# The two MLPs in an order written out by hand, with half of one more weight block as a Strassen product

## The chip, the cores and the metric

The kernel runs on one core of a Trainium2 chip. The metric is device time in microseconds: the median over executions of the whole kernel, inputs and outputs in HBM. Beside it there is a profile of one execution, from which all rows below are taken. The engines are called as the profile calls them: PE is TensorE (matmuls; PEld its weight loads), DVE VectorE, ACT ScalarE, POOL GpSimd, SP SyncE, which issues the loads.

## The reference

A model of two layers on 256 tokens of width 2048, all in fp32. Each layer adds an attention and then an MLP to the residual h: layer 0 a stick-breaking attention, layer 1 a native sparse attention with compressed, selected and windowed branches. The change concerns the MLPs alone:

```python
def sqrelu_mlp(h, w1, w2):
    return jnp.square(jax.nn.relu(h @ w1)) @ w2

h = h + sqrelu_mlp(rms_norm(h, mlp_norm_g[layer]), mlp_w1[layer], mlp_w2[layer])
```

w1 is 2048 x 8192, w2 is 8192 x 2048.

## The kernel before

**Precision.** A product in fp32 is made of three matmuls in fp32r. Each operand is split into a high part (a copy to fp32r, on ACT) and a low part (the difference, on DVE), and high x high, low x high and high x low are summed in PSUM. So each chunk of weights, 256 rows by 512 columns, 512 KB, is loaded to a `raw` tile by SP (`load`), split by ACT and DVE into `hi` and `lo` (`split`, lines 142 and 144; four buffers of each), and used by PE.

**Chunks.** Three kinds are told apart below. A chunk of the first product (`chunk_T`, line 206, "T") has 24 matmuls of 256 columns: the weights are the stationary operand, the normalized input xs (its halves xhi and xlo) moves. A plain chunk of the second product (`chunk_N`, line 173, "N") has 12 matmuls of 512 columns: the activations yhi and ylo are stationary, the weights move. A Strassen chunk of the second product (`chunk_S`, line 269, "S") does the same with seven half-size products instead of eight: 21 matmuls of 256 columns. For it DVE forms three sums of quarters of the weights (lines 245, 248, 249), ACT and DVE split three of the quarters (`shi` and `slo`, one buffer each, lines 247 and 250) and the four sums (lines 142 and 144 again). The activations' sums `ss` are made once, when the activations are made. The products of one S block fill four PSUM banks; `add_S` combines them into h with one ACT copy and seven DVE instructions (lines 293 to 302).

**Groups.** An MLP runs in four groups of 2048 hidden columns. In each, `group1` makes 32 T chunks (four blocks of 512 hidden columns, eight chunks each) and after each block the squared relu, its split into yhi and ylo, and the sums `ss`. Then `group2` multiplies by the matching rows of w2, in four blocks of 512 output columns: blocks 0 and 1 as N chunks, with block 2's eight S chunks put between them. Block 3's eight S chunks are put between the T chunks of the next group. In the last group blocks 0, 1 and 3 are plain and block 2 is S.

**Residual inputs.** When a block of h is finished, `next_x` prepares the next layer's input from it. It is a generator: first the squares of the block on ACT (`ssq`, line 349), then twice `make_x`: four transposes on PE (line 328), two ACT copies to xhi (line 333), two DVE instructions to xlo (line 335). `spawn` puts such a generator on a list with a rate, and `pump`, which each chunk calls twice (behind its hi matmuls and behind its lo matmuls), adds half the rate to a count and takes a step for every whole one. After the output projection of an attention, the `next_x` of its last block is still on that list when the MLP begins. `done` adds them at the end of layer 0's MLP; at the end of layer 1 it stores finished blocks of the output.

**Order.** Every engine runs its instructions in the order of its own queue. In most of the kernel the framework's scheduler chooses that order, from its own estimate of when things are ready, and may put an instruction ahead of others that the program emits earlier. In a block `with tc.manual_schedule(engines=...)` the order on the named engines is that in which the program emits. The kernel has one such block, the first stage (lines 508 to 571), where the first projections start; both MLPs are left to the scheduler.

**Loads.** `raw` tiles rotate over five buffers; within the MLPs every sixth load uses one more, `raw6`.

## Time and profile before

| | |
|---|---|
| median of 3 runs | 2145.69 us (2145.44 to 2146.96) |
| the profiled execution | 2144.79 us, of which its span is 2143.1 us |
| PE busy | 2136.4 us, 100% of the span |
| DVE busy | 1563.9 us, 73% |
| ACT busy | 1231.6 us, 57% |
| DMA | 190 GB/s mean |
| granted PE clock | 1.00 |

The MLP of layer 0 runs on PE from 391.7 us of the span, that of layer 1 from 1459.0 us to the end. In rows of a timeline the first number is the start and the second the length, in us; "x24" is a count of merged instructions, and a bracket gives the idle time before an instruction and what ended it. In rows of waits the numbers are the total, the count and the longest. Rows of the chain of waits have start, length, engine, tile and line.

### The profile page before, as it was taken

Reading aid. Unit: us, or ns where it says so; the run is one execution under the profiler, and the core shown is the slowest. Engines: PE = TensorE matmul, PEld = TensorE weight load, DVE = VectorE, ACT = ScalarE, POOL = GpSimd, SP = SyncE. Lnnn points to the kernel's source line nnn. Section 1 sums busy time; section 2 is a strip of 40 time slices with the busy share of each in tenths; the row PEclk is TensorE's granted clock in tenths of the full one; section 3 lists DMA queues with packets and bytes.
Section 4 is the critical chain, followed back from the end, with each engine's and each line's share of the span. In section 5 each row is a group of like instructions: output and inputs, shape, how many; then the busy total and the mean of one; then the engine's idle time right before and its main releaser. Section 6 shows DMA issues by size and latency. Waiting matters only on the chain.

```text
span 2143.1 us, 37272 instructions
## 1 busy us (share of the span) xinstructions
PE 2136.4 (100%) x14894; PEld 1973.4 (92%) x14894; DVE 1563.9 (73%) x2131; ACT 1231.6 (57%) x1653; POOL 45.2 (2%) x75
## 2 busy tenths in 40 slices
PE   9999999999999999999999999999999999999999
PEld 9999988998998999999898888889989989989998
DVE  5556556567878778778777888765678797788786
ACT  6555665555555555565555666655655555655653
POOL 0000000000000000000000111000000000000000
PEclk9999999999999999999999999999999999999999
DMA  7655556665665666665667654456656656656664
GB/s 240 210 172 177 158 180 186 186 195 188 207 202 186 205 197 203 217 197 186 194 185 217 169 145 136 149 177 187 197 170 215 205 188 213 197 189 210 204 195 149
DMA packets 260789, 406.34 MB, mean 190 GB/s; under 512 B 13188, under 2 KB 91912, under 8 KB 260616
## 3 DMA queue, kind: packets, MB, share of 16 engines
q1 hardware_dynamic: 259800, 403.52, 60.2%
q8 instruction: 116, 1.90, 0.4%
q10 hardware_dynamic: 816, 0.46, 0.1%
q14 instruction: 57, 0.47, 0.1%
HBM read 401.83 MB, written 2.10 MB: 188 GB/s over the span
## 4 chain that ended last, share of the span: by engine, by line
PE 98%; DVE 1%; DMA 0%; ACT 0%; issue 0%; POOL 0%; SPq 0%; DVEq 0%; ACTq 0%; POOLq 0%
PE acc L206 43%; PE acc L173 37%; PE att L269 12%; PE att L173 1%; PE att L328 1%; PE att L944 1%; DMA raw<-in_nsa_w_in_dram 0%; DVE lo L144 0%; PE att L655 0%; PE att L607 0%; PE att L882 0%; PE att L938 0%; PE att L884 0%; PE att L883 0%; PE att L936 0%; PE att L937 0%
## 5 line engine op out<-in xcount | busy, mean ns | idle before, releaser
L142 ACT ACTIVATE hi<-raw 128x1024 fp32r<-128x1024 f32 x639 | 676.0, 1060 | 576.1 <-PE acc L206 274.0
L144 DVE TENSOR_TENSOR lo<-raw,hi 128x1024 fp32r<-128x1024 f32 x639 | 776.6, 1222 | 252.9 <-ACT hi L142 241.3
L206 PE MATMUL acc<-xs,hi 128*128 128x256 f32 x5360 | 665.2, 277 | 0.0
L206 PEld LDWEIGHTS acc<-xs,hi 128*128 128x128 f32 x5360 | 634.4, 188 | 0.9
L206 PE MATMUL acc<-xs,lo 128*128 128x256 f32 x2680 | 359.3, 277 | 0.0
L206 PEld LDWEIGHTS acc<-xs,lo 128*128 128x128 f32 x2680 | 329.2, 188 | 0.0
L173 PE MATMUL acc<-hi,yhi 128*128 128x512 f32 x828 | 324.9, 393 | 0.0
L173 PE MATMUL acc<-hi,ylo 128*128 128x512 f32 x828 | 323.4, 391 | 0.0
L173 PE MATMUL acc<-lo,yhi 128*128 128x512 f32 x828 | 224.3, 392 | 0.0
L245 DVE TENSOR_TENSOR ts<-raw 128x512 f32<-128x512 f32 x112 | 77.4, 691 | 167.2 <-DMA raw<-in_mlp_w_dram 166.7
L142 ACT ACTIVATE hi<-ts 128x1024 fp32r<-128x1024 f32 x112 | 118.7, 1060 | 136.8 <-PE acc L173 67.8
L173 PEld LDWEIGHTS acc<-lo,yhi 128*128 128x128 f32 x828 | 154.7, 188 | 31.6
L173 PEld LDWEIGHTS acc<-hi,ylo 128*128 128x128 f32 x828 | 155.7, 188 | 29.5 <-DVE ylo L315 0.2
L173 PEld LDWEIGHTS acc<-hi,yhi 128*128 128x128 f32 x828 | 155.6, 188 | 29.5 <-ACT yhi L314 0.2
L173 PE MATMUL acc<-hi,xs 128*128 128x512 f32 x704 | 177.2, 392 | 0.0
L173 PEld LDWEIGHTS acc<-hi,xs 128*128 128x128 f32 x704 | 130.3, 188 | 26.1
L144 DVE TENSOR_TENSOR lo<-ts,hi 128x1024 fp32r<-128x1024 f32 x112 | 136.5, 1219 | 3.5 <-ACT hi L142 3.5
L247 ACT ACTIVATE shi<-raw 128x768 fp32r<-128x768 f32 x112 | 94.6, 845 | 54.8 <-PE att L269 34.5
L250 DVE TENSOR_TENSOR slo<-raw,shi 128x768 fp32r<-128x768 f32 x112 | 106.7, 953 | 4.8 <-PE att L269 4.8
L173 PE MATMUL acc<-lo,xs 128*128 128x512 f32 x352 | 97.1, 396 | 0.0
L269 PE MATMUL att<-hi,ss 128*128 128x256 f32 x672 | 94.4, 276 | 0.0
L269 PEld LDWEIGHTS att<-hi,ss 128*128 128x128 f32 x672 | 84.5, 188 | 0.0
(248 smaller groups left out, 2119.7 us busy)
## 6 DMA issues: line engine op xcount, KB each, us to landing
raw<-in_mlp_w_dram SPq DMA_DIRECT2D x512, 512.0 KB, 4.3
raw<-in_sb_w_qkv_dram SPq DMA_DIRECT2D x95, 512.0 KB, 3.9
raw<-in_nsa_w_in_dram SPq DMA_DIRECT2D x50, 512.0 KB, 3.8
raw<-in_sb_w_out_dram SPq DMA_DIRECT2D x32, 512.0 KB, 3.9
raw<-in_nsa_w_in_dram SPq DMA_DIRECT2D x64, 256.0 KB, 3.8
raw<-in_nsa_w_out_dram SPq DMA_DIRECT2D x32, 512.0 KB, 3.6
w1t<-in_nsa_cmp_w_dram SPq DMA_DIRECT2D x8, 512.0 KB, 4.0
h<-in_x_dram SPq DMA_DIRECT2D x8, 256.0 KB, 4.5
```

Of the source, the lines that this page charges most:

```text
L142: nc.scalar.activation(hi, raw, AF.Copy)
L144: nc.vector.tensor_tensor(lo, raw, hi.bitcast(F32), op=OP.subtract)
L173: mm = lambda a, b, k, t, s, e: nc.tensor.matmul(ps[t], a[:, k, t * P:(t + 1) * P], b, start=s, stop=e)
L206: nc.tensor.matmul(o, w, x[:, k0 + kk, :], start=s, stop=e, skip_group_check=True)
L245: nc.vector.tensor_tensor(ts[:, :2, :], flat[:, W:3 * W].rearrange("p (a n) -> p a n", a=2), b12, op=OP.subtract)
L247: nc.scalar.activation(hi, flat[:, :3 * W], AF.Copy)
L250: nc.vector.tensor_tensor(lo, flat[:, :3 * W], hi.bitcast(F32), op=OP.subtract)
L269: nc.tensor.matmul(ps[i], a, w, start=s, stop=e, skip_group_check=True)
L328: nc.tensor.transpose(ps[:, j * T + t * P:j * T + (t + 1) * P], h[:, t, (kp + j) * P:(kp + j + 1) * P], ident)
L944: nc.tensor.transpose(ptp[:w, j * P:(j + 1) * P], src(j), ident)
```

## The change

Both MLPs are put into a block of hand-written order. `group1` and `group2` with their generator give way to a list of steps (`plan`): chunks T, N and S, and the evaluations that belong to them, placed by the index of the plain chunk behind which they come. The evaluation of a block of hidden columns becomes four steps behind successive chunks: relu and square; the copy to yhi with the four DVE sums; the copy of the sums with ylo; the low half of the sums. A group but the last now has in its second half 20 plain chunks (block 0's eight N, the first block of the next group's T chunks, block 1's last four N) and 12 S chunks (block 1's first four, block 2's eight), and in its first half 24 T chunks beside block 3's eight S chunks. The last group keeps blocks 0, 1 and 3 plain and block 2 S. Block 1 therefore has two sums into h, one of each kind. Three further buffers take three of every eight loads (`more`), so raw tiles rotate over eight. The square is computed in place of the relu, the Strassen sum's temporary shares a buffer with the activations' sums, the squares' scratch tile has one buffer, and three output stores of layer 1 are issued from POOL instead of SP. `pump`, `chunk_T`, `chunk_N`, `chunk_S`, `make_x` and `next_x` stay as they are.

The functions that are taken away are those shown above; their bodies are left out here.

```diff
--- before.py
+++ after.py
@@ -35,6 +35,7 @@
 ST = 32
 SK = 2 * ST + NCMP
 GATES = 3 * NH
+JUNK = 1
 SLOPES = [2.0 ** (-8.0 * (i + 1) / NH) for i in range(NH)]
 
 
@@ -144,14 +145,14 @@
         nc.vector.tensor_tensor(lo, raw, hi.bitcast(F32), op=OP.subtract)
         return hi, lo
 
-    sixth = None
+    more = None
     loads = 0
 
     def load(src, k0, nk, n0, nn):
         nonlocal loads
         loads += 1
-        if sixth is not None and loads % 6 == 0:
-            raw = sixth.tile([P, nk, nn], F32, name="raw6", bufs=1)
+        if more is not None and loads % 8 in (2, 5, 7):
+            raw = more.tile([P, nk, nn], F32, tag="more", name="more", bufs=3)
         else:
             raw = wraw.tile([P, nk, nn], F32, tag="raw", name="raw")
         nc.sync.dma_start(
@@ -287,7 +288,7 @@
     def add_S(nb, bs, ps, pool, scale):
 
         W = NB // 2
-        uv = pool.tile([P, 4, W], F32, tag="pre", name="uv", bufs=1)
+        uv = pool.tile([P, 4, W], F32, tag="sums", name="uv", bufs=1)
         u, v = uv[:, :2, :], uv[:, 2:, :]
         hb = [h[:, t, nb * NB:(nb + 1) * NB] for t in range(NT)]
         nc.scalar.activation(u[:, 0, :], ps[0], AF.Copy)
@@ -345,7 +346,7 @@
             ssq_t[layer] = small.tile([P, NT, n], F32, tag="ssq", name="ssq")
         w = D // n
         for t in range(NT):
-            j = small.tile([P, NB], F32, tag="junk", name="junk")
+            j = small.tile([P, NB], F32, tag="junk", name="junk", bufs=JUNK)
             nc.scalar.activation(
                 j[:, :w], h[:, t, i * w:(i + 1) * w], AF.Square, accum_out=ssq_t[layer][:, t, i:i + 1]
             )
@@ -417,80 +418,159 @@
     def mlp(l, layer, junk, done, last=None):
         w1, w2 = mlp_w1[l], mlp_w2[l]
         ss = far(junk, KD * 4 * P, "ss").rearrange("p (a k i n) -> p a k i n", a=2, k=KD // 2, i=4)
-        factor = junk.tile([P, T], F32, name="factor", bufs=1)[:, :NT]
+        factor = junk.tile([P, 64], F32, name="factor", bufs=1)[:, :NT]
+        NK, NF, NG, KB = KD // KC, D // NB, DFF // D, NB // P
+        banks, part = {}, {}
 
         def factors():
             yield
             r = make_rstd(layer)
             nc.vector.tensor_tensor(factor, r, r, op=OP.mult)
 
-        def in_S(fg, nb):
...
-        def group1(fg, beside_w1):
...
-        def group2(fg, end):
...
+        def chunk1(fg, fb, i):
+            if i == 0:
+                banks["T", fb] = [bank(acc, "acc") for _ in range(KB // 2)]
+            chunk_T(banks["T", fb], w1, i * KC, fg * D + fb * NB, i == 0, i == NK - 1)
+
+        def relu(fb):
+            a = part["s", fb] = junk.tile([P, KB, T], F32, tag="sq", name="sq", bufs=1)
+            for j in range(0, KB, 2):
+                nc.scalar.activation(
+                    a[:, j:j + 2, :], banks["T", fb][j // 2].rearrange("p (m t) -> p m t", m=2), AF.Relu
+                )
+
+        def square(fb):
+            s = part["s", fb]
+            nc.scalar.activation(s, s, AF.Square)
+
+        def high(fb):
+            k, s = fb * KB, part["s", fb]
+            nc.scalar.activation(yhi[:, k:k + KB, :], s, AF.Copy)
+            sv = s.rearrange("p (j kk) t -> p j kk t", kk=2)
+            a1, a2 = [[sv[:, :, kk, t * P:(t + 1) * P] for kk in (1, 0)] for t in range(NT)]
+            q = part["q", fb] = junk.tile([P, 2, 4, P], F32, tag="sums", name="sums", bufs=1)
+            nc.vector.scalar_tensor_tensor(q[:, :, 0, :], a2[0], -1.0, a2[1], op0=OP.mult, op1=OP.subtract)
+            nc.vector.tensor_tensor(q[:, :, 2, :], a1[0], a2[0], op=OP.subtract)
+            nc.vector.tensor_tensor(q[:, :, 1, :], a2[1], q[:, :, 2, :], op=OP.subtract)
+            nc.vector.tensor_tensor(q[:, :, 3, :], a1[1], q[:, :, 1, :], op=OP.subtract)
+
+        def low(fb):
+            k, s = fb * KB, part["s", fb]
+            nc.scalar.activation(ss[:, 0, k // 2:k // 2 + 2], part["q", fb], AF.Copy)
+            nc.vector.tensor_tensor(ylo[:, k:k + KB, :], s, yhi[:, k:k + KB, :].bitcast(F32), op=OP.subtract)
+
+        def low7(fb):
+            k = fb * KB
+            o = ss[:, :, k // 2:k // 2 + 2]
+            nc.vector.tensor_tensor(o[:, 1], part["q", fb], o[:, 0].bitcast(F32), op=OP.subtract)
+
+        def chunk2(fg, nb, i, first, end, turn, by_token=False):
+            if first:
+                banks["N", nb] = [bank(acc, "acc") for _ in range(NT)]
+            chunk_N(banks["N", nb], w2, fg * KD + i * KC, nb * NB, first, end, yhi, ylo, koff=fg * KD,
+                    by_token=by_token, turn=turn)
+
+        def chunk7(fg, nb, i, first, end):
+            if first:
+                banks["S", nb] = banks_S(att, "att")
+            chunk_S(banks["S", nb][1], w2, fg * KD + i * KC, nb * NB, first, end, yhi, ylo, ss[:, 0], ss[:, 1],
+                    koff=fg * KD)
+
+        def sum2(nb):
+            add_h(nb, banks["N", nb], factor)
+
+        def sum7(nb):
+            add_S(nb, *banks["S", nb], junk, factor)
+
+        def plan():
+
+
+            def merge(plain, after):
+                for j, c in enumerate(plain):
+                    yield c
+                    yield from after.pop(j, ())
+                assert not after
+
+            def do(f, *args):
+                return lambda: f(*args)
+
+            def Ts(fg, fb):
+                return [("T", fg, fb, i) for i in range(NK)]
+
+            def Ns(fg, nb, ks=range(NK)):
+                return [("N", fg, nb, i, i == ks[0], i == ks[-1]) for i in ks]
+
+            def Ss(fg, nb, at, after, ks=range(NK)):
+                for i, j in zip(ks, at):
+                    after.setdefault(j, []).append(("S", fg, nb, i, i == ks[0], i == ks[-1]))
+
+            def put(after, j, *fs):
+                after.setdefault(j, []).extend(fs)
+
+            def stages(after, j, fb, stash=False):
+                if not stash:
+                    put(after, j, do(relu, fb))
+                put(after, j, do(square, fb))
+                for i, f in enumerate((high, low, low7)):
+                    put(after, j + 1 + i, do(f, fb))
+
+            half = NK // 2
+            for fg in range(NG):
+                after = {}
+                if fg == 0:
+                    plain = sum([Ts(0, fb) for fb in range(NF)], [])
+                    for fb in range(NF - 1):
+                        stages(after, fb * NK + NK + 2, fb)
+                else:
+                    plain = sum([Ts(fg, fb) for fb in range(1, NF)], [])
+                    put(after, 2, do(sum7, 2))
+                    put(after, 3, do(sum2, 1))
+                    Ss(fg - 1, 3, (3, 5, 7, 10, 13, 15, 18, 21), after)
+                    stages(after, 8, 0, True)
+                    stages(after, 13, 1)
+                    stages(after, 18, 2)
+                yield from merge(plain, after)
+                after = {}
+                if fg:
+                    put(after, 1, do(sum7, 3))
+                stages(after, 2, NF - 1)
+                if fg < NG - 1:
+                    plain = Ns(fg, 0) + Ts(fg + 1, 0) + Ns(fg, 1, range(half, NK))
+                    Ss(fg, 1, (4, 5, 6, 7), after, range(half))
+                    put(after, 10, do(sum7, 1))
+                    put(after, 11, do(sum2, 0))
+                    Ss(fg, 2, (12, 13, 14, 15, 16, 17, 18, 19), after)
+                    put(after, 18, do(relu, 0))
+                else:
+                    plain = Ns(fg, 0) + Ns(fg, 1) + Ns(fg, 3)
+                    put(after, 10, do(sum2, 0))
+                    Ss(fg, 2, (4, 6, 8, 10, 11, 13, 15, 17), after)
+                    put(after, 17, do(sum2, 1))
+                    put(after, 18, do(sum7, 2), *[do(done, n, (att, "att")) for n in range(3)])
+                    if last is None:
+                        put(after, 23, do(sum2, 3), do(done, 3, (att, "att")))
+                yield from merge(plain, after)
 
         spawn(factors(), 1)
-        NK = KD // KC
-        for fg in range(DFF // D):
-            group1(fg, in_S(fg - 1, 3) if fg else None)
-            group2(fg, fg == DFF // D - 1)
+        with tc.manual_schedule(engines={mybir.EngineType.PE, mybir.EngineType.DVE, mybir.EngineType.Activation,
+                                         mybir.EngineType.SP}):
+            steps = list(plan())
+            for n, c in enumerate(steps):
+                if callable(c):
+                    c()
+                    continue
+                follower = next((d[0] for d in steps[n + 1:] if not callable(d)), None)
+                if c[0] == "T":
+                    chunk1(*c[1:])
+                elif c[0] == "S":
+                    chunk7(*c[1:])
+                elif last is not None and c[1:3] == (NG - 1, 3):
+                    fg, nb, i, first, end = c[1:]
+                    chunk2(fg, nb, i, first, i == NK - 2, False, end)
+                else:
+                    chunk2(*c[1:], turn=follower in ("T", "S"))
+            if last is not None:
+                add_out(3, banks["N", 3], last, factor)
 
 
     with tc.tile_pool(name="sbp", bufs=2) as sp:
@@ -690,13 +770,13 @@
     nc.vector.tensor_copy(peT, ppe[:, :2 * CL])
 
     with tc.tile_pool(name="m0p", bufs=2) as mp:
-        wsum = sixth = mp
+        wsum = more = mp
 
         def done0(nb, pool):
             spawn(next_x("nsa", nb, G_NSA, pool), 1.5)
 
         mlp(0, "m0", mp, done0)
-        sixth = None
+        more = None
 
 
 
@@ -842,7 +922,7 @@
 
         def heads(pv, t, n):
 
-            sq = small.tile([P, n, P], F32, tag="junk", name="hsq")
+            sq = small.tile([P, n, P], F32, tag="junk", name="hsq", bufs=JUNK)
             nc.scalar.activation(sq, pv, AF.Square, scale=rstd[:, t:t + 1])
             s = small.tile([P, HG], F32, tag="hs", name="hs", bufs=4)
             nc.vector.tensor_reduce(s[:, :n], sq, axis=AX.X, op=OP.add)
@@ -1082,12 +1162,12 @@
         out_proj(nsa_w_out[0], "m1", G_M1)
 
     with tc.tile_pool(name="m1p", bufs=2) as mp:
-        wsum = sixth = mp
+        wsum = more = mp
         ov = out[0].rearrange("(t p) d -> p t d", p=P)
 
         def done1(nb, pool):
             if nb < D // NB - 1:
-                nc.sync.dma_start(ov[:, :, nb * NB:(nb + 1) * NB], h[:, :, nb * NB:(nb + 1) * NB])
+                nc.gpsimd.dma_start(ov[:, :, nb * NB:(nb + 1) * NB], h[:, :, nb * NB:(nb + 1) * NB])
 
         mlp(1, "m1", mp, done1, ov)
```

More of the change, by code (lines that the diff above doesn't have):

```diff
@@ L425, in factors @@
             nc.vector.tensor_tensor(factor, r, r, op=OP.mult)
-        def in_S(fg, nb):
-            for i in range(NK):
-                if i == 0:
-                    bs, s = banks_S(att, "att")
-                chunk_S(s, w2, fg * KD + i * KC, nb * NB, i == 0, i == NK - 1, yhi, ylo, ss[:, 0], ss[:, 1],
-                        koff=fg * KD)
-                if i == NK - 1:
-                    add_S(nb, bs, s, junk, factor)
-                yield
-        def group1(fg, beside_w1):
-            step = lambda: next(beside_w1)
-            for fb in range(D // NB):
-                ps = [bank(acc, "acc") for _ in range(NB // P // 2)]
-                proj_T(ps, w1, fg * D + fb * NB, then={2: step, 5: step} if beside_w1 else {})
-                k, n = fb * (NB // P), NB // P
-                a = junk.tile([P, n, T], F32, tag="pre", name="pre", bufs=1)
-                for j in range(0, n, 2):
-                    nc.scalar.activation(a[:, j:j + 2, :], ps[j // 2].rearrange("p (m t) -> p m t", m=2), AF.Relu)
-                s = junk.tile([P, n, T], F32, tag="sq", name="sq", bufs=1)
-                nc.scalar.activation(s, a, AF.Square)
-                nc.scalar.activation(yhi[:, k:k + n, :], s, AF.Copy)
-                nc.vector.tensor_tensor(ylo[:, k:k + n, :], s, yhi[:, k:k + n, :].bitcast(F32), op=OP.subtract)
-                sv = s.rearrange("p (j kk) t -> p j kk t", kk=2)
-                a1, a2 = [[sv[:, :, kk, t * P:(t + 1) * P] for kk in (1, 0)] for t in range(NT)]
-                q = junk.tile([P, 2, 4, P], F32, tag="sums", name="sums", bufs=1)
-                nc.vector.scalar_tensor_tensor(q[:, :, 0, :], a2[0], -1.0, a2[1], op0=OP.mult, op1=OP.subtract)
-                nc.vector.tensor_tensor(q[:, :, 2, :], a1[0], a2[0], op=OP.subtract)
-                nc.vector.tensor_tensor(q[:, :, 1, :], a2[1], q[:, :, 2, :], op=OP.subtract)
-                nc.vector.tensor_tensor(q[:, :, 3, :], a1[1], q[:, :, 1, :], op=OP.subtract)
-                split_evac(ss[:, 0, k // 2:k // 2 + 2], ss[:, 1, k // 2:k // 2 + 2], q)
@@ L462, in group2 @@
-        def group2(fg, end):
-            blocks = (0, 1, 3) if end else (0, 1)
-            side, si = in_S(fg, 2), 0
-            for j in range(len(blocks) * NK):
-                nb, i = blocks[j // NK], j % NK
-                if i == 0:
-                    ps = [bank(acc, "acc") for _ in range(NT)]
-                out = last is not None and end and nb == 3
-                aside = si < NK and j >= 4 + (1.75 if end else 1.4) * si
-                chunk_N(ps, w2, fg * KD + i * KC, nb * NB, i == 0, i == NK - (2 if out else 1), yhi, ylo,
-                        koff=fg * KD, by_token=out and i == NK - 1,
-                        turn=aside or (not end and j == len(blocks) * NK - 1))
-                if i == NK - 1:
-                    if out:
-                        add_out(nb, ps, last, factor)
-                        return
-                    add_h(nb, ps, factor)
-                    if end and nb == 3:
-                        done(nb, (att, "att"))
-                if aside:
-                    next(side)
-                    si += 1
-                    if si == NK and end:
-                        for n in range(3):
-                            done(n, (att, "att"))
```

## The prediction

> **What bounds the kernel now.** I read the page first, then the waits of TensorE, the chain of waits in order of time, and last the table by stretches over one MLP group of layer 0.
>
> ```profile
> span 2143.1 us, 37272 instructions
> ...
> PE 2136.4 (100%) x14894; PEld 1973.4 (92%) x14894; DVE 1563.9 (73%) x2131; ACT 1231.6 (57%) x1653; POOL 45.2 (2%) x75
> ```
>
> ```profile
> PE att L515 <- POOL ident masks.py:199: 1.6, 1, 1.6
> PE att L789 <- DVE hs L784: 0.5, 1, 0.5
> PE att L836 <- DVE kc L831: 0.4, 1, 0.4
> PE acc L534 <- ACT hi L527: 0.2, 1, 0.2
> ```
>
> ```profile
> 400.98 78.90 PE acc L206 x696
> 479.88 13.63 PE acc L173 x60
> ```
>
> In the next, each row is a stretch: its length, then busy time of PE, its weight loads, DVE, ACT and POOL, the granted clock and the DMA share.
>
> ```profile
> 543.00:649.10 106.10, 106.10 (x938) 106.10 (x937) 82.00 (x102) 60.22 (x65) 0.00 (x0) 1.00 0.63 203
> 649.10:712.00 62.90, 62.90 (x362) 55.20 (x362) 55.07 (x73) 36.27 (x39) 0.00 (x0) 1.00 0.61 201
> ```
>
> TensorE is busy all the time and its four waits sum to 2.7 us, none of them in an MLP. So a matmul taken out of an MLP is time won, and any new wait of TensorE is time lost one for one; nothing absorbs it. The prices of a chunk on TensorE follow from these rows. A first-product chunk T (24 matmuls): 78.90/29 = 2.721 us. A plain second-product chunk N (12 matmuls of 512): 13.63/5 = 2.726. The stretch 543.00 to 649.10 holds 32 T and 8 Strassen chunks S (21 matmuls of 256): S = (106.10 - 87.06)/8 = 2.38. The next one holds 16 N and 8 S: S = (62.90 - 43.62)/8 = 2.41, transitions included. The clock is 1.00 in both.
>
> **The matmuls that go.** In three of four groups of each MLP, four of block 1's eight N chunks become S: 2 x 3 x 4 = 24 chunks, each 2.726 - 2.40 = 0.326 us shorter, in all -7.8 us (bounds -7.6 and -8.3 with S at 2.41 and 2.38). T chunks moved among the second products keep their price.
>
> [...]
>
> **VectorE.** An S chunk costs it more than an N chunk, and it must do so in less TensorE time. From the timeline of VectorE late in layer 1, where it runs back to back, and at the last Strassen sum, and from the chain, TensorE's five last plain chunks:
>
> ```profile
> 2107.58 0.69 DVE L245 TENSOR_TENSOR ts<-raw 128x512 f32<-128x512 f32 x1 [1.47 <-DMA raw<-in_mlp_w_dram]
> ...
> 2111.11 2.35 DVE L144 TENSOR_TENSOR lo<-raw,hi 128x1024 fp32r<-128x1024 f32 x2
> 2113.38 1.41 DVE L386 SCALAR_TENSOR_TENSOR h<-acc,factor,h 128x512 f32<-128x512 f32 x2
> ...
> 2122.30 0.75 DVE L298 SCALAR_TENSOR_TENSOR h<-att,factor,h 128x512 f32<-128x512 f32 x1 [0.54 <-PE att L269]
> 2123.05 1.23 DVE L144 TENSOR_TENSOR lo<-raw,hi 128x1024 fp32r<-128x1024 f32 x1
> 2124.20 0.42 DVE L294 TENSOR_TENSOR uv<-att,uv 128x256 f32<-128x256 f32 x1
> ...
> 2127.30 1.22 DVE L144 TENSOR_TENSOR lo<-raw,hi 128x1024 fp32r<-128x1024 f32 x1
> ```
>
> ```profile
> 2122.72 13.61 PE acc L173 x60
> ```
>
> One S chunk takes 2111.11 - 2107.58 = 3.53 us, a plain split (2113.38 - 2111.11)/2 = 1.135, a Strassen sum 0.75 + (2127.30 - 2124.20) = 3.85. A group's second half now has 20 plain and 12 S chunks and one sum more: VectorE 55.07 + 4 x 1.135 + 4 x 3.53 + 3.85 = 77.6 us, TensorE 20 x 2.724 + 12 x 2.40 = 83.3. That is 93%, from 88%. In hand order VectorE also idles where the chunk's second split waits for ScalarE and where the single slo buffer is freed by the S chunk before. Walking one pair (plain, S) of 5.12 us through the three engines: slo can start 2.1 us after the previous S starts on TensorE (17 of its 21 matmuls have then read it), the split of the sums ends 2.0 later, the next plain split 1.1 later, the next three sums 1.6 later; at 6.8 VectorE waits until 5.12 + 2.1 = 7.2. It keeps step, 0.4 us to spare in each pair, and each split is ready about 3 us before TensorE reads it. So I take 0 for this; the bounds are 0 and the DVE rival below.
>
> A Strassen sum placed in program order stops every split behind it until TensorE has finished the S product. Before the inner ones stand three plain chunks whose splits are done (8.2 us of cover against 3.85 + 1.135, and 3.53 where an S comes next: 8.5 beside 10.9 of TensorE work). The one at the end of the last group has only chunk 18: S ends at 2122.72, the sum runs to about 2126.5, chunk 19's lo is ready at 2127.7; TensorE reaches its lo matmuls at 2122.72 + 2.73 + 1.82 = 2127.3. Before, the row at 2123.05 shows that split put ahead of the sum. Cost 0.4 us, twice: +0.8 (bounds 0 and 1.1 each).
>
> **The residual inputs inside the ordered region.** This decides the sign. The region fixes the order of TensorE, VectorE, ScalarE and SyncE to the order in which the program emits, and `pump` still emits pieces of `next_x` there. A chunk emits its splits, then its matmuls, then from its second pump `make_x`: four transposes on TensorE and two copies to xs on ScalarE. The next chunk's hi copy is emitted behind these, so ScalarE can't split ahead: it waits for transposes which stand behind a whole chunk of TensorE work. What this looks like can be seen in the first stage of this same kernel, which is ordered by hand already (SyncE, TensorE, ScalarE, and the loads' median time to landing):
>
> ```profile
> 21.47 4.53 SPq L157 DMA_DIRECT2D raw<-in_sb_w_qkv_dram  x2
> ```
>
> ```profile
> 33.72 0.60 PE L328 MATMUL att<-ident,h 128*128 128x128 f32 x4
> 34.07 2.08 PE L206 MATMUL acc<-xs,hi 128*128 128x256 f32 x16
> ```
>
> ```profile
> 34.35 0.84 ACT L333 ACTIVATE xs<-att,gT 128x256 fp32r<-128x256 f32 x2 [2.37 <-PE att L328]
> 35.08 1.06 ACT L142 ACTIVATE hi<-raw 128x1024 fp32r<-128x1024 f32 x1
> ```
>
> ```profile
> raw<-in_sb_w_qkv_dram SPq DMA_DIRECT2D x95, 512.0 KB, 3.9
> ```
>
> The weights split at 35.08 were asked for at 21.47 and such a load lands after 3.9 us, yet ScalarE sat idle 2.37 us in front of xs. There the loop has one more chunk, already split, between the transposes and that split's use, so TensorE went on at 34.07. In the MLP no such chunk stands between. Today the scheduler lets ScalarE run ahead (its timeline at the MLP's start, and the chain there and at layer 0's end):
>
> ```profile
> 393.18 0.19 ACT L349 ACTIVATION_READ_ACCUMULATOR junk<-h 128x1 f32 x1
> 393.85 1.06 ACT L142 ACTIVATE hi<-raw 128x1024 fp32r<-128x1024 f32 x1 [0.48 <-PE acc L206]
> 396.54 1.07 ACT L142 ACTIVATE hi<-raw 128x1024 fp32r<-128x1024 f32 x1 [1.63 <-PE acc L206]
> 397.84 0.84 ACT L333 ACTIVATE xs<-att,gT 128x256 fp32r<-128x256 f32 x2 [0.23 <-PE att L328]
> ```
>
> ```profile
> 391.70 5.67 PE acc L206 x48
> 397.37 0.44 PE att L328 x4
> ...
> 1060.41 0.93 PE acc L173 x4
> 1061.34 0.44 PE att L328 x4
> ```
>
> There are four hi buffers, so a split waits until TensorE has read that of the fourth chunk before it. The two at 393.85 and 396.54 waited for first products (L206), the MLP's own first two chunks, and are those of its fifth and sixth chunk; both stand before the first xs. With the new order the third chunk's hi comes after that xs. Price of one hole, from the ordered stage: xs starts 0.63 after the transposes, the next ScalarE instruction 0.73 later, hi takes 1.06, in all 2.42; TensorE would have gone on 0.35 after the transposes. The hole is 2.07 us. VectorE's xlo and lo fit beside the hi matmuls.
>
> How many: at each MLP's start `next_x` of block 3 is left over, rate 1, so its two `make_x` come from the second pumps of chunks 1 and 2 (today's transposes at 397.37 confirm the place): 2 x 2 holes. The squares of `ssq` go ahead of chunk 1's hi and end at 393.18 + 0.19 = 393.37; that hi ends 1.06 later, at 394.43, and TensorE wants it at 391.70 + 2.72 = 394.42: no hole. At the end of layer 0, `done` spawns at rate 1.5 after chunk 18: squares after 19, two `make_x` in chunk 20 and two in chunk 22, one from each pump. Today's rows from 1060.41 show this rhythm; the second of each pair, after the lo matmuls, is followed by chunk 21's and 23's hi: 2 holes. Together 6 x 2.07 = +12.4 us (bounds 0 and 2.72, a whole chunk, each).
>
> [...]
>
> **Edits at nothing.** Eight raw buffers instead of six: loads wait less, and no load is on TensorE's path today. Reusing the tiles sq, sums and junk adds waits within ScalarE and VectorE of about one instruction, inside the 3 us lead. The three stores of finished blocks go from SyncE's queue to GpSimd's, which has nothing else to do then; issued at about 2127, each takes 5.9 us in today's profile, with 12 us of matmuls and the last 128 KB stores still to come:
>
> ```profile
> out_dram<-h SPq DMA_DIRECT2D x3, 512.0 KB, 5.9
> ```
>
> If GpSimd needed several microseconds to issue them it would still be covered; past 6 us the tail would grow by the excess.
>
> **Sum.** -7.8 + 0.8 + 12.4 = +5.4 us on the profiled execution's 2144.79 (its span 2143.1 and 1.7 around it), 2150.2. The median of the three runs shown is 0.9 above that execution: 2151.1; I say 2151.
>
> **The rivals.** (a) The holes do not come: faster. For it: TensorE is full everywhere, so -7.8 is then real; it decides once at most one of the six holes opens, as when ScalarE gets the next hi ahead of xs because emitted pieces of `next_x` escape the order. Against it: the ordered stage's rows. 2144.79 - 7.8 + 0.9 = 2137.9. (b) Some holes: only the four at the starts of the MLPs, 8.3 us, which cancels the matmuls: 2146.2, no change. (c) VectorE becomes the bound of the second halves. It decides when its idling there passes 83.3 - 77.6 = 5.7 us; with 1 us lost in each of 12 S chunks each half takes 89.6, six halves +38 us: 2189. For it: 93%. Against it: the walk above, and the first halves, where eight T chunks go and VectorE falls to 82.00 - 9.1 = 72.9 of 84.3 us, enough to catch up. A mild case, one missed lead of 3 us in a few halves, gives 2155 to 2160. (d) The new S chunks bring no saving because T, N and S now alternate: the 2.38 against 2.41 above shows what a transition costs, 0.03 us; one in and one out of each bound this at 24 x 0.06 = 1.4 us and stays inside the others.
>
> **How the numbers follow.** Forecast, six holes: 0.56, with 2148.5 to 2154 as its own range (S at 2.38 or 2.41, holes of 1.7 to 2.5). (a) 0.18, (b) 0.16, (c) 0.10. Two runs of this kernel can't be told apart within 0.2%, 4.3 us: slower means above 2150.0, faster below 2141.4. A fifth of the forecast's weight lies under 2150.0; so slower 0.45 + 0.10 = 0.55, no change 0.11 + 0.16, less a little of (b) that goes to the faster side, 0.25, faster 0.20. The range runs from (a), 2137, to 2155; it leaves out most of (c) and the edge of (a).
>
> **What would show it.** The waits of TensorE should list L206 <- ACT hi about four times and L173 <- ACT hi twice, near 2.1 us each, at the third and fourth chunk of each MLP and before the last group's chunks 21 and 23 of layer 0; transposes at L328 stand just before each. Matmuls of S should number 136 x 21 instead of 112 x 21 and TensorE's busy time fall by about 8. VectorE in a second half should be near 78 of 83 us. If those chunks follow the transposes without a gap, the argument on emission order is wrong; if gaps stand at S chunks with lo or slo as releaser, (c) is at work.

## The result, and the profile after

The changed kernel takes 2157.33 us (median of 6, 2154.9 to 2163.41) beside 2145.66 us before: 1.0057 times, 95% interval 1.0042 to 1.0071. It is slower, as forecast, but by 11.7 us where 5.4 were expected, and it lies above the range. The profiled execution took 2155.24 us, 10.45 more than that of before.

The page of the changed kernel, first lines, and its waits of TensorE from 0.5 us on (total, count, longest). Lines have moved: the hi split is now L143, the lo split L145, N L174, T L207, S L270, the transposes L329, the copies to xs L334.

```profile
span 2153.5 us, 37647 instructions
...
PE 2134.2 (99%) x15110; PEld 1979.8 (92%) x15110; DVE 1654.2 (77%) x2269; ACT 1232.2 (57%) x1683; POOL 45.5 (2%) x78
```

```profile
PE acc L207 <- ACT hi L143: 7.7, 5, 1.9
PE acc L174 <- ACT hi L143: 2.9, 2, 1.9
PE att L595 <- POOL ident masks.py:199: 1.6, 1, 1.6
PE acc L174 <- DVE lo L145: 1.1, 2, 0.6
PE att L898 <- DVE a L889: 1.0, 1, 1.0
PE acc L207 <- ACT xs L334: 0.6, 1, 0.6
```

TensorE issues 216 matmuls more, 24 x 9, as an S chunk has 21 and an N chunk 12. The waits of the MLPs, absent before, are those in the first, second and fourth row; the sixth is at the handover to layer 1. Where the first row comes from is seen in TensorE's timeline at the start of layer 0's MLP, with ScalarE below it:

```profile
397.51 0.60 PE L329 MATMUL att<-ident,h 128*128 128x128 f32 x4
399.98 2.10 PE L207 MATMUL acc<-xs,hi 128*128 128x256 f32 x16 [1.87 <-ACT hi L143]
401.91 1.07 PE L207 MATMUL acc<-xs,lo 128*128 128x256 f32 x8
402.82 0.60 PE L329 MATMUL att<-ident,h 128*128 128x128 f32 x4
405.30 2.91 PE L207 MATMUL acc<-xs,hi 128*128 128x256 f32 x16 [1.87 <-ACT hi L143]
408.00 1.90 PE L207 MATMUL acc<-xs,lo 128*128 128x256 f32 x8
409.71 2.03 PE L207 MATMUL acc<-xs,hi 128*128 128x256 f32 x16
```

```profile
398.14 0.84 ACT L334 ACTIVATE xs<-att,gT 128x256 fp32r<-128x256 f32 x2 [3.54 <-PE att L329]
398.87 1.05 ACT L143 ACTIVATE hi<-more 128x1024 fp32r<-128x1024 f32 x1
```

Two holes, behind the transposes, each until a hi that stands behind xs on ScalarE. From transposes to matmul it is 399.98 - 397.51 = 2.47 us where 0.35 is the undisturbed step, so a hole costs 2.12. But there is more. The T chunk at 399.98 takes 402.82 - 399.98 = 2.84 up to the next transposes, while the one behind the second hole takes 409.71 - 405.30 = 4.41. Two stretches of 3 us there (length, busy time of PE, weight loads, DVE, ACT, POOL, then the granted clock) say why:

```profile
405.00:408.00 3.00, 2.70 (x16) 2.70 (x17) 2.81 (x5) 3.00 (x4) 0.00 (x1) 0.72 0.24 24
408.00:411.00 3.00, 3.00 (x20) 3.00 (x20) 2.27 (x3) 1.14 (x2) 0.69 (x1) 0.71 0.88 298
```

The granted clock has fallen to 0.72 and 0.71, while TensorE was at work for 2.70 and 3.00 of the 3 us. In steps of 0.2 us it reads 0.50 from 406.40 to 409.60, and 3 x 0.28 + 3 x 0.29 = 1.71 us lost over the two stretches is 3.4 us at 0.50. At layer 1's start that happens behind both holes: 1477.85 - 1473.52 = 4.33 and 1484.83 - 1480.46 = 4.37 us:

```profile
1473.52 2.82 PE L207 MATMUL acc<-xs,hi 128*128 128x256 f32 x16 [1.87 <-ACT hi L143]
1476.14 1.91 PE L207 MATMUL acc<-xs,lo 128*128 128x256 f32 x8
1477.85 0.74 PE L329 MATMUL att<-ident,h 128*128 128x128 f32 x4
1480.46 2.86 PE L207 MATMUL acc<-xs,hi 128*128 128x256 f32 x16 [1.87 <-ACT hi L143]
1483.12 1.91 PE L207 MATMUL acc<-xs,lo 128*128 128x256 f32 x8
1484.83 2.06 PE L207 MATMUL acc<-xs,hi 128*128 128x256 f32 x16
```

A T chunk is 2.72 us, so the three slow ones cost 1.69 + 1.61 + 1.65 = 4.95 us. At the end of layer 0 the other holes and the Strassen sums' waits:

```profile
1062.31 1.20 PE L174 MATMUL acc<-lo,yhi 128*128 128x512 f32 x4 [0.56 <-DVE lo L145]
...
1066.54 0.60 PE L329 MATMUL att<-ident,h 128*128 128x128 f32 x4
1069.01 0.50 PE L174 MATMUL acc<-hi,yhi 128*128 128x512 f32 x1 [1.87 <-ACT hi L143]
...
1075.10 1.47 PE L329 MATMUL att<-ident,h 128*128 128x128 f32 x12
1077.57 0.50 PE L174 MATMUL acc<-hi,yhi 128*128 128x512 f32 x1 [1.00 <-ACT hi L143]
```

The ledger of the profiled execution: 7.5 us saved by the S chunks (by the eighth experiment below); four holes of 2.12 at the starts, 8.5; one of 2.12 at the end, and one of which 1.0 idle is left, since eight more transposes moved into it; 1.1 for the two sums; 0.8 in which T waits for xs or for a hi behind the squares (the 0.6 of the sixth row, and 7.7 - 4 x 1.87 = 0.2 of the first); 4.95 at the lower clock. In all +11.0 against 10.45 measured, 0.5 too much. Without the clock it is +6.0.

### The profile page after: what moved, and what is told of

Its sections match the earlier page's. It is cut to its first block, busy times and chain, and to the rows that moved or that the text cites. A ratio compares the mean times of both kernels' runs of the same rounds, so it can differ in the third digit from the quotient of the medians.

```text
span 2153.5 us, 37647 instructions
## 1 busy us (share of the span) xinstructions
PE 2134.2 (99%) x15110; PEld 1979.8 (92%) x15110; DVE 1654.2 (77%) x2269; ACT 1232.2 (57%) x1683; POOL 45.5 (2%) x78
## 5 line engine op out<-in xcount | busy, mean ns | idle before, releaser
L145 DVE TENSOR_TENSOR lo<-raw,hi 128x1024 fp32r<-128x1024 f32 x486 | 590.1, 1221 | 210.8 <-ACT hi L143 201.5
L143 ACT ACTIVATE hi<-raw 128x1024 fp32r<-128x1024 f32 x486 | 509.8, 1054 | 291.5 <-PE acc L174 122.4
L207 PE MATMUL acc<-xs,hi 128*128 128x256 f32 x5360 | 667.3, 277 | 8.3 <-ACT hi L143 7.7
L207 PEld LDWEIGHTS acc<-xs,hi 128*128 128x128 f32 x5360 | 635.9, 188 | 10.2 <-ACT hi L143 8.8
L207 PE MATMUL acc<-xs,lo 128*128 128x256 f32 x2680 | 361.4, 278 | 0.0
L207 PEld LDWEIGHTS acc<-xs,lo 128*128 128x128 f32 x2680 | 331.4, 189 | 0.0
L174 PE MATMUL acc<-hi,yhi 128*128 128x512 f32 x732 | 287.1, 392 | 2.9 <-ACT hi L143 2.9
L174 PE MATMUL acc<-hi,ylo 128*128 128x512 f32 x732 | 285.6, 390 | 0.0
L143 ACT ACTIVATE hi<-ts 128x1024 fp32r<-128x1024 f32 x136 | 144.3, 1061 | 186.8 <-DVE ts L250 185.3
L174 PE MATMUL acc<-lo,yhi 128*128 128x512 f32 x732 | 198.5, 392 | 1.1 <-DVE lo L145 1.1
L145 DVE TENSOR_TENSOR lo<-more,hi 128x1024 fp32r<-128x1024 f32 x129 | 157.4, 1220 | 45.9 <-ACT hi L143 45.2
L145 DVE TENSOR_TENSOR lo<-ts,hi 128x1024 fp32r<-128x1024 f32 x136 | 166.4, 1223 | 23.9 <-ACT hi L143 22.8
L174 PE MATMUL acc<-hi,xs 128*128 128x512 f32 x704 | 177.8, 392 | 0.0
L174 PEld LDWEIGHTS acc<-hi,yhi 128*128 128x128 f32 x732 | 137.4, 188 | 29.4 <-ACT hi L143 3.3
L174 PEld LDWEIGHTS acc<-lo,yhi 128*128 128x128 f32 x732 | 136.5, 188 | 29.8 <-DVE lo L145 2.0
L174 PEld LDWEIGHTS acc<-hi,ylo 128*128 128x128 f32 x732 | 137.5, 188 | 26.0 <-DVE ylo L316 0.2
L143 ACT ACTIVATE hi<-more 128x1024 fp32r<-128x1024 f32 x129 | 135.7, 1052 | 36.3 <-PE acc L207 21.1
L174 PEld LDWEIGHTS acc<-hi,xs 128*128 128x128 f32 x704 | 130.1, 188 | 26.0
L248 ACT ACTIVATE shi<-raw 128x768 fp32r<-128x768 f32 x73 | 61.8, 846 | 103.3 <-PE att L270 103.3
L270 PE MATMUL att<-hi,ss 128*128 128x256 f32 x816 | 114.6, 276 | 0.0
L248 ACT ACTIVATE shi<-more 128x768 fp32r<-128x768 f32 x63 | 53.2, 844 | 97.0 <-PE att L270 97.0
L270 PEld LDWEIGHTS att<-hi,ss 128*128 128x128 f32 x816 | 102.6, 188 | 0.0
```

The source lines that it names most:

```text
L143: nc.scalar.activation(hi, raw, AF.Copy)
L145: nc.vector.tensor_tensor(lo, raw, hi.bitcast(F32), op=OP.subtract)
L174: mm = lambda a, b, k, t, s, e: nc.tensor.matmul(ps[t], a[:, k, t * P:(t + 1) * P], b, start=s, stop=e)
L207: nc.tensor.matmul(o, w, x[:, k0 + kk, :], start=s, stop=e, skip_group_check=True)
L248: nc.scalar.activation(hi, flat[:, :3 * W], AF.Copy)
L270: nc.tensor.matmul(ps[i], a, w, start=s, stop=e, skip_group_check=True)
```

## The experiments

**1. Splits one chunk ahead.** The order in which the program emits is changed, and nothing else: before the matmuls of a chunk, the load and the splits of the chunk after it are emitted (those of S are cut out of `chunk_S` as `split_S`).

```diff
...
+                here = order.index(n)
+                for m in order[here:here + 1 + (1)]:
+                    if m not in ready:
+                        ready[m] = prepare(m)
+                w = ready.pop(n)
                 if c[0] == "T":
-                    chunk1(*c[1:])
+                    chunk1(*c[1:], w)
...
```

> The changed kernel, but inside the ordered region each chunk's load and splits are emitted ahead of the matmuls of the chunk before it (one chunk of look-ahead); chunks, sums and everything else are the same. Theory A (the loss is the six holes of TensorE behind make_x, two small ones behind the last Strassen sums, and half clock for some microseconds after the paired holes): all of these go, TensorE's clock is 1.00 throughout, and the 24 chunks that became Strassen's show: 2145.7 - 7.8 = 2138 us, and the runs lie within 2 us of each other. Theory B (hand order itself, or VectorE at over 90%, costs the time): little changes, 2150 us or more.

Measured 2135.73 us (2135.05 to 2136.74), 0.9952 of before [0.9939, 0.9964], 2.3 us below what theory A gave. From its page, and TensorE's three longest waits:

```profile
span 2134.3 us, 37626 instructions
...
PE 2126.3 (100%) x15110; PEld 1974.2 (92%) x15110; DVE 1654.4 (78%) x2269; ACT 1231.6 (58%) x1683; POOL 46.3 (2%) x78
```

```profile
PE att L618 <- POOL ident masks.py:199: 1.6, 1, 1.6
PE att L921 <- DVE a L912: 1.0, 1, 1.0
PE acc L637 <- ACT hi L630: 0.7, 1, 0.7
```

None of these is in an MLP, nor any shorter one. The whole loss hangs on where a chunk's load and splits stand relative to the pieces of `next_x` and to the sums, and this version beats both kernels.

**2 and 3. The same at the starts alone, and at the ends alone.**

```diff
-                for m in order[here:here + 1 + (1)]:
+                for m in order[here:here + 1 + (here < 8)]:
```

```diff
-                for m in order[here:here + 1 + (1)]:
+                for m in order[here:here + 1 + (here >= len(order) - 24)]:
```

> The look-ahead only for the first eight chunks of each MLP. Theory A: the four holes at the two starts go, 4 x 2.1 = 8.4 us, and with them the half clock that follows them, about 5 us: 2157.3 - 13.4 = 2144 us. If the low clock had another cause (such as the burst of splits after a hole), the gain is only 8.4: 2149.

> The look-ahead only for the last 24 chunks of each MLP. Theory A: the two holes at the end of layer 0 (2.1 us each), the 1.0 us one before chunk 23's neighbour, and the two waits behind the last Strassen sums (0.74 each) go, together 5 to 6 us; the holes at the starts and the half clock stay: 2151.5 us, with the same spread between runs as the changed kernel. Theory B: no difference.

At the starts: 2142.38 us (2141.44 to 2143.84), ratio 0.9983 [0.9974, 0.9992]. At the ends: 2151.5 (2147.85 to 2155.23), 1.0022 [1.0012, 1.0031]. From 2157.33 the one takes away 14.9 us and the other 5.8, together 20.8 beside the 21.6 of both at once: the two places add up, and the starts weigh far more than their four holes (8.5). The spread, too, sits at the starts: 2.4 us where they are mended, 7.4 where they are not. In the second (mean granted clock of the profiled execution 0.999) the clock fell behind the first hole that was left at the end of layer 0. Its matmuls of 512 columns then start every 0.43 us, and every 0.23 us again from 1067.21 on, 3.6 us later:

```profile
1062.77 0.50 PE L174 MATMUL acc<-hi,yhi 128*128 128x512 f32 x1 [1.88 <-ACT hi L143]
...
1063.63 0.63 PE L174 MATMUL acc<-hi,ylo 128*128 128x512 f32 x1
1064.06 0.63 PE L174 MATMUL acc<-hi,yhi 128*128 128x512 f32 x1
...
1067.21 0.39 PE L174 MATMUL acc<-hi,yhi 128*128 128x512 f32 x1
1067.44 0.40 PE L174 MATMUL acc<-hi,ylo 128*128 128x512 f32 x1
```

**4. The holes kept busy.** Behind each chunk that ended with a `make_x` stand 18 identity transposes whose results nobody uses.

```diff
...
+                if made:
+                    made.clear()
+                    warm = bank(att, "att")
+                    for _ in range(18):
+                        nc.tensor.transpose(warm[:, :P], ident, ident)
```

> The changed kernel with 18 transposes of the identity (about 2 us of TensorE work, to a PSUM bank that nobody reads) behind each chunk that ended with a make_x, so TensorE is busy in the holes but nothing starts earlier. Theory A: the holes cost the same, but the clock stays at 1.00, so 5 us come back and the spread between runs shrinks to 2 us: 2152 us. If the slow chunks after a hole do not come from idling, the time stays at 2157 and their matmuls still take 1.5 times as long.

2153.69 us (2150.34 to 2155.39), 1.0027 [1.0018, 1.0037]; 3.6 below the changed kernel by medians, 4.8 by the profiled executions (2150.48 and 2155.24), beside the 4.95 of the ledger. The place of the first fall, same window:

```profile
405.00:408.00 3.00, 3.00 (x27) 2.85 (x26) 2.71 (x5) 3.00 (x5) 0.11 (x1) 1.00 0.19 27
```

TensorE does no more useful work in it than in the hole, the next T chunk starts no earlier, and the clock stays at 1.00. The mean granted clock is 1.000 in all nine executions, where it is 0.997 or 0.998 in all six of the changed kernel. So the fall comes of the idle time, not of the splits or the loads there. But the spread of 5 us stayed, which the theory had put down to the clock: there was something else.

**5. Filling only every other hole.**

The lines are those that differ from the fourth experiment:

```diff
...
+                fill = made and not filled[-1:] == [1]
                 if made:
                     made.clear()
+                    filled.append(1 if fill else 0)
+                if fill:
                     warm = bank(att, "att")
...
```

> The changed kernel with 18 identity transposes (about 2 us of TensorE, results not used) behind every other chunk that ended with transposes of the next layer's input, so that of the two holes at the start of an MLP the first is filled and the second stays. If the clock falls only where two holes stand close together: granted clock 1.00 at both starts, as with both filled (2153.7 there). If one hole of 2 us is enough: granted clock below 0.9 for some 4 us behind the second hole of at least one start, and 2155 to 2158.

2158.04 us (2154.82 to 2159.31), 1.0057 [1.0042, 1.0072]. One hole was enough for a fall. With TensorE busy from the MLP's start and a single hole of 1.88 us, the clock fell at layer 0's start, where the 16 hi matmuls take 3.29 us; at layer 1's, behind a hole of 1.87, they take 2.15 and there was no fall. The execution's mean granted clock is 0.999, as one fall of 1.65 us gives:

```profile
405.42 3.29 PE L207 MATMUL acc<-xs,hi 128*128 128x256 f32 x16 [1.88 <-ACT hi L143]
408.51 1.55 PE L207 MATMUL acc<-xs,lo 128*128 128x256 f32 x8
...
1478.51 2.15 PE L207 MATMUL acc<-xs,hi 128*128 128x256 f32 x16 [1.87 <-ACT hi L143]
1480.50 1.10 PE L207 MATMUL acc<-xs,lo 128*128 128x256 f32 x8
1481.44 2.05 PE L207 MATMUL acc<-xs,hi 128*128 128x256 f32 x16
1483.33 1.10 PE L207 MATMUL acc<-xs,lo 128*128 128x256 f32 x8
1484.27 2.05 PE L207 MATMUL acc<-xs,hi 128*128 128x256 f32 x16
```

Yet this execution is as long as that of the changed kernel (span 2153.1 and 2153.5) with one fall in place of three. The last rows hold an answer: with no fall there a T chunk takes 1484.27 - 1481.44 = 2.83 us, not 2.72. The groups of lines over 413 to 483 us, granted clock 1.00 in both, show the same (count, busy time, mean ns of one, idle time before them), first the third experiment's profiled execution (2154.05), then the changed kernel's:

```profile
L207 PE MATMUL acc<-xs,hi 128*128 128x256 f32 x399 | 51.1, 281 | 0.0
```

```profile
L207 PE MATMUL acc<-xs,hi 128*128 128x256 f32 x413 | 51.0, 276 | 0.0
```

Such a stretch begins with the T chunks behind the holes and ends before the first S chunk, some 29 chunks later: 29 x 0.107 = 3.1 us. The third experiment's execution had one at each start, 6.2 us, as much as lies between it and that kernel's shortest, 2154.05 - 2147.85; but the shortest has no profile, so that this is the reason is argued only. Over the profiles of the changed kernel and of the third and fifth experiments, four of ten starts with an open hole had such a stretch; in the seven profiles with splits ahead at the starts, none of fourteen. In the fifth experiment two of the four executions had a mean granted clock of 1.000, the longest (2159.31) among them, so the clock alone doesn't make an execution long.

**6 and 7. Two more executions of the changed kernel with a profile**, to test this sum.

> The changed kernel itself, one more execution with a profile, to see in what its executions differ (2154.9 to 2163.4). In the profiles so far a hole at the start of an MLP was followed by one or both of two things. The granted clock falls to about half for some 3.4 us (1.65 us lost). Or the 29 first-product chunks behind the holes keep a pace of 2.83 us a chunk in place of 2.72 at a granted clock of 1.00, until the first chunk of Strassen's form (29 x 0.107 = 3.1 us lost). The first profile of this kernel, 2155.24, had three clock falls and no such stretch. Theory: an execution takes 2155.24 + 1.65 x (clock falls - 3) + 3.1 x (stretches), within 0.8 us. Rival: the spread is the chip's own, seen in all kernels alike; then falls and stretches don't add up to the difference between the executions.

> The same once more. Theory: 2155.24 + 1.65 x (clock falls - 3) + 3.1 x (stretches of slow pace), within 0.8 us, with at least one of the two counts unlike that of another look whose time differs by more than 1.5 us. Rival: times differ and the counts don't.

The first of the two took 2155.96 us, with two falls (both at layer 0's start) and one stretch of 29 T chunks: the sum says 2155.24 - 1.65 + 3.1 = 2156.7. The other took 2154.39, with two falls (one at each start) and no stretch at a start: 2153.6. Both are within the 0.8 allowed, but at its edge and on opposite sides: the two differ by 1.6 us where the sum gives 3.1. Part of that lies in 11 T chunks at the slow pace at the beginning of layer 1's attention (1093.5 to 1124.3 us) in the second, 1.2 us which the sum doesn't count. So the sum is supported and not shown to 0.8 us.

The longest executions, up to 2163.41, have no profile. Their clock doesn't explain them: 2163.41 and 2156.17 both have a mean granted clock of 0.997, and a fall, some 3.4 us at half clock, is 0.0008 of the mean, so rounding leaves room for hardly more than one fall, some 2 us (an estimate), of the 7.2 between them. That the rest is the slow pace is argued only. Nor is the rival out: the kernel before, which has no such holes, ran from 2144.93 to 2151.32 us over the 26 executions beside the first four experiments.

**8. The S chunks alone.** Splits ahead, and block 1 plain again.

```diff
-                    plain = Ns(fg, 0) + Ts(fg + 1, 0) + Ns(fg, 1, range(half, NK))
-                    Ss(fg, 1, (4, 5, 6, 7), after, range(half))
-                    put(after, 10, do(sum7, 1))
+                    plain = Ns(fg, 0) + Ts(fg + 1, 0) + Ns(fg, 1)
                     put(after, 11, do(sum2, 0))
-                    Ss(fg, 2, (12, 13, 14, 15, 16, 17, 18, 19), after)
+                    Ss(fg, 2, (12, 13, 14, 15, 17, 19, 21, 23), after)
```

> The changed kernel with its splits emitted one chunk ahead, and with block 1 of the middle groups in plain products again (24 chunks of Strassen's form fewer, the number that the kernel before has). By the prediction's first term each such chunk is 2.726 - 2.40 = 0.33 us of TensorE, so the kernel without them must stand 7.8 us above the one with splits ahead (2135.7 there): 2143.5, and no wait in the MLPs. Rival: VectorE, which has less to do without them, was what set the pace of the second halves; then taking them away costs less than 7.8, down to nothing (2136 to 2140).

2143.05 us (2142.64 to 2144.71), 0.9988 [0.9979, 0.9997], span 2142.3: the 24 chunks are worth 2143.05 - 2135.73 = 7.3 us by medians and 2142.3 - 2134.3 = 8.0 by spans. Of the 8.0, 7.5 lie in the MLPs (681.16 - 677.44 from layer 0's first T to the first T behind its MLP, and 683.51 - 679.77 from layer 1's first T to the end); the rest is layer 1's attention, where this execution has 12 T chunks at the slow pace. Without the 24 chunks the new order with splits ahead is a little faster than the scheduler's, by 2.9 us beside the kernel before in the same session (2145.94); where these lie stays open.

**9 and 10. Buffers and stores.** Splits ahead with six raw buffers, and with the three stores of layer 1 back on SyncE.

```diff
-        if more is not None and loads % 8 in (2, 5, 7):
-            raw = more.tile([P, nk, nn], F32, tag="more", name="more", bufs=3)
+        if more is not None and loads % 6 == 0:
+            raw = more.tile([P, nk, nn], F32, tag="more", name="more", bufs=1)
```

```diff
-                nc.gpsimd.dma_start(ov[:, :, nb * NB:(nb + 1) * NB], h[:, :, nb * NB:(nb + 1) * NB])
+                nc.sync.dma_start(ov[:, :, nb * NB:(nb + 1) * NB], h[:, :, nb * NB:(nb + 1) * NB])
```

> Splits one chunk ahead as before in these runs, but six raw buffers in place of eight. If the buffers are no part of the gain: 2135.7, within 1.5 us, and no TensorE wait that begins with a late transfer. If the earlier loads need the two more buffers: transfers land late and splits wait for them, some 2 us at each place where four chunks of 2.4 us follow one another, 2138 to 2145.

> Splits one chunk ahead, and the three stores of the finished blocks in layer 1's MLP issued by SyncE again, as in the kernel before, in place of GpSimd. If the queue of the stores costs nothing, as the prediction has it: 2135.6, within 1 us. If a store's wait for its sum holds the loads behind it on SyncE: the raw buffers run dry at the end of layer 1's MLP and a split waits for a load there, 2136.5 to 2140.

Six buffers: 2135.49 us (2135.06 to 2136.75), no change. Stores on SyncE: 2144.62 (2143.3 to 2146.11), 8.9 us lost, more than the 1 to 4 us expected for that case. SyncE's wait in front of the first store, and TensorE's wait at the end of layer 1:

```profile
SPq L1193 <- DVE h L391: 17.7, 1, 17.7
```

```profile
PE acc L174 <- ACT hi L143: 6.5, 1, 6.5
```

In program order the store stands on SyncE until its block of h is finished, 17.7 us, and the loads of the last chunks behind it. The hole is 6.5 us; the mean granted clock is 0.998 or 0.997 in all ten executions, where it is 1.000 with splits ahead alone.

**11 and 12. Eight S chunks more**, half of block 1 in the last groups too; first with two pairs of S chunks side by side (the first line for block 2), then evenly spread (the second, with `done` at rate 2.5). The sums and `done` move with them.

```diff
-                    plain = Ns(fg, 0) + Ns(fg, 1) + Ns(fg, 3)
+                    plain = Ns(fg, 0) + Ns(fg, 1, range(half, NK)) + Ns(fg, 3)
+                    Ss(fg, 1, (4, 5, 6, 7), after, range(half))
...
-                    Ss(fg, 2, (4, 6, 8, 10, 11, 13, 15, 17), after)
+                    Ss(fg, 2, (10, 11, 12, 13, 13, 14, 14, 15), after)
+                    Ss(fg, 2, (9, 10, 11, 12, 13, 14, 15, 16), after)
```

> Splits one chunk ahead, and half of block 1 in Strassen's form in the last group of each MLP too (8 chunks more): 8 x 0.33 = 2.6 us less TensorE. If TensorE alone sets the pace: 2133.1. If VectorE, which must then make the operands of 12 such chunks beside 20 plain ones at the end of the MLP too, or the sums that close block 2 hold up TensorE there: no gain or up to 4 us lost (2136 to 2140), with waits on the low parts or on the sums at the end of each MLP.

> Half of block 1 in Strassen's form in the last groups too, as in the run before, but with never two such chunks side by side, and with the transposes of the next layer's input handed out 2.5 to a chunk. 8 x 0.33 = 2.6 us less TensorE than with splits ahead alone (2135.6). If the loss of the run before came from the pairs, where the second chunk's operands wait for the first chunk's buffer: 2133 to 2134. If VectorE and ScalarE can't feed one such chunk to each plain one beside the transposes: 2136 to 2141, with waits on the low or high parts all along the last groups.

2140.8 and 2140.0 us: 5.1 and 4.3 us above splits ahead alone. (Neither computes what the reference does any more; which of the moves does that was not found, so they are read for their waits alone.) The second, over the last group of layer 0:

```profile
1000.00:1060.00 60.00, 58.47 (x368) 51.99 (x367) 56.39 (x75) 29.76 (x33) 0.00 (x0) 1.00 0.56 178
```

VectorE is busy for 56.4 of 60 us and TensorE no longer full: six waits of S chunks for ACT's hi, whose sums VectorE makes, 2.9 us over both MLPs. The six chunks take 3.1 to 3.4 us in place of 2.39, 4.8 us in all, more than the 2.6 that the eight chunks were to save. Side by side or spread, there is no room for these; the rival of the prediction that VectorE becomes the bound begins here.

## Why the prediction came out as it did

**The matmuls that go:** right. -7.8 forecast, -7.5 in the MLPs of the eighth experiment, -7.3 by its medians.

**VectorE at nothing:** right. A second half was to have 77.6 us of VectorE in 83.3 of TensorE. The changed kernel's second group:

```profile
653.52:736.80 83.28, 83.28 (x590) 77.43 (x589) 74.98 (x97) 47.65 (x54) 0.00 (x0) 1.00 0.63 192
```

83.28 it is, with VectorE at 75.0 and TensorE never waiting at an S chunk, so rival (c) did not come. VectorE has 2.6 us less there than worked out and 2.9 more in the first half behind it (75.8 where 72.9 was worked out). That the measured time falls into (c)'s mild case, 2155 to 2160, is luck. The nearness of the VectorE bound was right all the same: the last two runs cross it.

**The Strassen sums at the end of the last groups:** right in place, 0.56 us of idle time each where 0.4 was said. (The times of rivals (a) and (b) leave this term out; with its 0.8 us they would be 2138.7 and 2147.0.)

**The residual inputs inside the ordered region:** right in cause, place and number. Four holes at T behind transposes, two at N in layer 0; 2.12 us where 2.07 was worked out, and the last half filled. The experiments with splits ahead take the holes away by moving nothing but the loads and splits. Not seen were 0.6 us at the handover to the next layer, where T waits for xs, and 0.2 for the hi behind the squares.

**The step that failed** is the price of one hole. It was taken as its idle time, with "The clock is 1.00 in both" read off stretches in which TensorE never stopped, and nothing asked what the clock does when it stops. In its place the runs show a fall of the clock behind seven of twelve holes at a start (three behind the four such holes in the first profile, two in each later one of this kernel), 1.65 us each, and in some executions 29 T chunks at the slower pace, 3.1 us. The falls alone are 3.3 to 5.0 us over the sum and a stretch 3.1 more. That the idle time brings the fall is shown by the fourth experiment; what brings the slower pace stays open, and with it a part of the spread.

What decides whether a hole brings a fall was not shown: holes of 1.87 us brought it at some starts and not at others, in the same kernel. The fall lasted 3.4 us in the first profile, and in the second experiment the slow matmuls lasted 3.6.

**Edits at nothing:** eight buffers, right. The stores on GpSimd cost nothing, as said, but the text missed what they avoid: in hand order on SyncE they would have cost 8.9 us.

## What to carry to other kernels

When a region is put in hand order, every piece that background generators emit there becomes a fixed place in a queue: emit the splits of the next chunk before the matmuls of this one (21.6 us here), and put no store that must wait for its data on a queue that also loads (8.9 us here). On a TensorE that is always busy, price a new hole at more than its length: behind seven of the twelve holes of 1.87 us at the starts here the clock was near 0.50 for some 3.4 us, 1.65 us lost each, and in some executions the next 29 T chunks took 2.83 us each in place of 2.72. A quick test is to fill the hole with useless matmuls; if the time falls, the hole had cost more than itself.

## What the runs showed of the hardware that was not expected

Behind a TensorE hole of 1.87 us the granted clock fell to 0.50 for 3.4 us, and a T chunk took 4.33 to 4.41 us instead of 2.72 (first profile); behind five of the twelve such holes at the starts of the changed kernel's three profiles it did not fall. With the hole filled by identity transposes the mean granted clock stayed at 1.000 in nine executions of nine.

Two paces at one granted clock, 1.00: T chunks of the same 24 matmuls ran at 2.72 us or at 2.83 us (means of 276 and 281 ns, starts 113 and 118 ns apart) for 29 chunks on end. The slower one also came without a hole: in the kernel before, nine T chunks in layer 1's attention (1088 to 1111 us) have the mean of 281 ns, and the first two of layer 1's MLP run at 2.82 us, and after four transposes the pace is the faster one (eight lo matmuls 1.07 us, where they were 1.10):

```profile
1458.85 2.05 PE L206 MATMUL acc<-xs,hi 128*128 128x256 f32 x16
...
1461.67 2.05 PE L206 MATMUL acc<-xs,hi 128*128 128x256 f32 x16
1464.50 0.60 PE L328 MATMUL att<-ident,h 128*128 128x128 f32 x4
1464.85 2.07 PE L206 MATMUL acc<-xs,hi 128*128 128x256 f32 x16
1466.76 1.07 PE L206 MATMUL acc<-xs,lo 128*128 128x256 f32 x8
```

What sets the pace was not found. Here it changed behind four transposes; in the fifth experiment chunks before and behind 18 of them ran at the slower one, 2.83 us.
